# RMS norms over features: sums by f32r matmuls with a block of minus ones, roots by logarithm and exponential

## Chip, cores and metric

The kernel runs on one NeuronCore (one of eight) of a Trainium2 chip. The metric is the device time of one execution in microseconds (us), the median of several runs; less is better.

## What is computed

Two sequences of 512 tokens with 1024 features go through two layers (a grouped 2-D Fourier mixing, then grouped-query attention with axial rotary positions), each followed by a squared-ReLU MLP with 4096 hidden units, and a final norm. Everything is float32. Each mixer, each MLP and the output has an RMS norm over the features in front:

```python
def rms_norm(x, g):
    x32 = x.astype(jnp.float32)
    y = x32 * lax.rsqrt(jnp.mean(x32 * x32, axis=-1, keepdims=True) + EPS)
    return (y * g.astype(jnp.float32)).astype(x.dtype)

def sq_relu_mlp(h, w_up, w_down):
    a = jnp.maximum(h @ w_up, 0)
    return (a * a) @ w_down

def trunk(x, ...):
    for i in range(DEPTH):
        j = i // N_MIXERS
        if i % N_MIXERS == 0:
            x = x + fourier_mix(rms_norm(x, fourier_norm[j]), fourier_w_out[j])
        else:
            x = x + gqa_attention(rms_norm(x, attn_norm[j]), ...)
        x = x + sq_relu_mlp(rms_norm(x, mlp_norm[i]), mlp_w_up[i], mlp_w_down[i])
    return rms_norm(x, final_norm)
```

In attention the queries and keys of each head have an RMS norm of their own, over 128 features.

## The kernel before

The residual is held in SBUF with the features on partitions and the tokens along the free axis: for each sequence q eight tiles `xt(q, fo)` of 128 features by 512 tokens. A product in float32 precision is made of three f32r matmuls: both operands are split into a high part (a cast on ScalarE, `split`, line 86) and a low part (a subtraction on VectorE, line 87), and the products high x high, high x low and low x high add up in PSUM (`mm3`, lines 81 to 83; `product`, line 940, for the MLP).

The MLP uses a Strassen-like scheme: `Blocks` holds normalised pieces of both sequences (`b11`, `b21`, `b22`) and their sums and differences (`t1` to `t4`). `first_product` goes over pairs of weight blocks; for the first few (`AHEAD`) pairs only the products with the plain pieces run (`pair.first` with sequence 0, `pair.second`), while the second sequence's norm is finished, and `rest` then makes the products with the sums. `second_product` is the way down, from line 1131.

A norm over features needs a sum over partitions. Before the change it runs so:

- `square` (line 173) squares each feature tile on ScalarE (line 178) and adds it on GpSimd (line 182) into `acc[q]`; one tile can stand `apart`.
- `sums` (line 185) multiplies each block of 128 tokens of `acc` as the stationary operand with two columns of ones (line 191), in float32. The sums lie with tokens on partitions, one column for each block.
- `rsqrt_steps` (line 136) takes the reciprocal root of these few columns: a scaled copy (line 141), Sqrt on ScalarE (142), a reciprocal (143), a square (144) and one Newton step in two combined operations (145, 146).
- `spread` (line 195) transposes each column, broadcast to 128 columns, back with TensorE (line 199), so that each partition holds the row of factors, and copies it from PSUM (line 200).
- `Blocks.norm` (line 238) or `OutT.write` (line 1873) multiplies the scaled pieces (`gain`, lines 225 and 1862) by that row.

`Blocks` does this for both sequences in layer 0 (after the Fourier mixing: lines 884 and 887 for sequence 0, in `first_product` at lines 1069 and following for sequence 1) and in layer 1 (lines 1809 and following, and again `first_product`). `OutT` does it for the final norm of sequence 0 (`oa`, four token blocks) and of half of sequence 1 (`ob`, two blocks); the rest of sequence 1 (`oc`, `oe`) is transposed first and uses sums along the free axis (`Out`). Two more users of `sums` are the per-token scales of attention (`token_scale`, line 1402). `norm_rope` (line 1465) makes the norms of heads, with `rsqrt_steps` on VectorE or `log_steps` on GpSimd. Sqrt and Exp come from different tables on ScalarE; tables are loaded at lines 352, 1702 and 1741.

All engines take their instructions in the order that the program gives in these stretches (`manual_schedule`) or that a scheduler with added dependencies (`behind`) gives elsewhere. SyncE issues most loads and the spills; spills of the plain pieces are issued by ScalarE.

Of the kernel before, what the change touches and what calls it, by code (L numbers as in the profile page):

```python
# [44 lines left out]
def trunk_kernel(ctx, tc, x_in, xt_in, y_out, tables, rope, gfour, gcol, grow, gfin,  # L45
# [86 lines left out]
    def rsqrt(out, ss, n, inv, room=None):  # L132
        for step in rsqrt_steps(out, ss, n, inv, room=room):
            step()
# [16 lines left out]
    def log_steps(out, ss, n, inv):  # L151

        v, s, r, t = [small(n)[:, :n] for _ in range(4)]
        return [
            lambda: nc.vector.tensor_scalar(v, ss, inv, EPS, ALU.mult, ALU.add),
            lambda: nc.scalar.activation(s, ss, AF.Ln, scale=inv, bias=eps[:, :1]),
            lambda: nc.scalar.activation(r, s, AF.Exp, scale=-0.5),
            lambda: nc.vector.tensor_mul(t, r, r),
            lambda: nc.vector.scalar_tensor_tensor(t, t, -0.5, v, ALU.mult, ALU.mult),
            lambda: nc.vector.scalar_tensor_tensor(out, t, 1.5, r, ALU.add, ALU.mult),  # L160
        ]
# [23 lines left out]
    def sums(q, n=NT):  # L185

        o = ps()
        parts = [acc[q]] + ([apart.pop(q)] if q in apart else [])
        for t in range(n):
            for i, x in enumerate(parts):  # L190
                nc.tensor.matmul(o[:, 2 * t : 2 * t + 2], x[:, t * P : (t + 1) * P], ones,  # L191
                                 start=i == 0, stop=i == len(parts) - 1)
        return o[:, 0 : 2 * n : 2], o[:, 64:]

    def spread(r, n=NT):

        o, rows = ps()[:, : n * P], tm()
        for t in range(n):
            nc.tensor.transpose(o[:, t * P : (t + 1) * P], r[:, t : t + 1].broadcast_to([P, P]), ident)  # L199
        nc.scalar.copy(rows[:, : n * P], o)  # L200
        return rows
# [12 lines left out]
    class Blocks:  # L214
# [12 lines left out]

        def root(self, q):
            self.r[q] = small()
            ss, room = sums(q)  # L230
            rsqrt(self.r[q][:, :NT], ss, NT, 1.0 / D, room)

        def spread(self, q):
            self.rows[q] = spread(self.r[q])
# [140 lines left out]
    nc.vector.memset(f32(filler), 1.0)  # L375
    def cosT(c):
        return tabs[2 * c][:, :516].rearrange("p (a b) -> p a b", a=2)
# [355 lines left out]
    with tc.manual_schedule(engines={ET.PE, ET.Activation, ET.DVE, ET.Pool, ET.SP}):  # L733
# [116 lines left out]
        g1.chain(2, 6)  # L850
        even(4)
# [24 lines left out]
        for fo in range(KC):  # L876
            e, = even_outs(1, [fo])
            even_add(1, fo, e)
            if fo < 4:
                for i in range(2 * fo, 2 * fo + 2):  # L880
                    blocks.gain(0, i)
                if fo != 2:
                    put_away(0, fo)
            if fo == 2:
                blocks.root(0)
            if fo == 3:
                blocks.spread(0)
            if 3 < fo:
                blocks.first(fo - 4)
            if 5 < fo:  # L890
                blocks.first_lo(fo - 6)
# [53 lines left out]
    def first_product(l, blocks, rows, ahead):  # L945
# [122 lines left out]
        for p in range(AHEAD):  # L1068
            if p == 4:
                blocks.spread(1)  # L1070
            pair = pairs[p]
            if p < len(rows):
                pair.row = rows[p]
            else:
                pair.load()
                pair.split_row()
                if p == 3 and wo_added:
                    behind(pair.low, wo_added[0])
            pair.first()
            if p == 3:  # L1080
                blocks.root(1)
            if p > 0:
                pair.second()
            if p == 1:
                pairs[0].second()
            if p > 3:
                for _ in range(3):
                    next(todo)
            if p == 5:
                pairs[0].load_sums()  # L1090
                pairs[0].sums_13()
                pairs[0].sum_2()
            if p == 6:
                pairs[0].split_23()
# [307 lines left out]
    def token_scale(q):  # L1402
        r = sm.tile([P, NT], F32, tag="rs", name=nm("rs"), bufs=2)
        ss, room = sums(q)
        rsqrt(r, ss, NT, 1.0 / D, room)
# [49 lines left out]
    def norm_rope(raw, nh, table, ts, outs, ss=None, step=None, eng=nc.vector, scale=None):  # L1455
# [9 lines left out]
        steps = (log_steps if eng is nc.gpsimd else rsqrt_steps)(r[:, :n], ss[:, :n], n, 1.0 / HD)  # L1465
# [234 lines left out]
    with tc.manual_schedule(engines={ET.Activation}):  # L1700
        o = qkv(1, 1, 2, ws[1])
        tc.keep_in_program_order(nc.scalar.preload_act_table_set("natural_log_exp_and_others"))
# [12 lines left out]
    for n in range(1, len(heads) + 1):  # L1715
# [14 lines left out]
        last = nxt[-1] if nxt else last  # L1730
# [10 lines left out]
    behind(nc.scalar.activation(one[:, :1], last[:, :1], AF.Sqrt), both[0])  # L1741

# [14 lines left out]
    with tc.manual_schedule(engines={ET.PE}):  # L1757
# [38 lines left out]
        o, lows = {}, []  # L1796
        for j, (m, i) in enumerate(turn()):
# [11 lines left out]
            if j == 0:  # L1809
# [24 lines left out]
    class Out:  # L1834
# [9 lines left out]
        def root(self, i):  # L1844

            more = small(1)[:, 0:1]
            steps = rsqrt_steps(self.r, self.ss[:, i : i + 1], 1, 1.0 / D, more)
# [5 lines left out]
    class OutT:  # L1853


        def __init__(self, q, n):
            self.q, self.n, self.r, self.y = q, n, small(n), []
# [7 lines left out]
        def root(self):  # L1865
            ss, room = sums(self.q, self.n)
            rsqrt(self.r[:, : self.n], ss, self.n, 1.0 / D, room)

        def spread(self):
            self.rows = spread(self.r, self.n)[:, : self.n * P]  # L1870
# [15 lines left out]
    with tc.manual_schedule(engines={ET.PE, ET.Activation, ET.DVE, ET.Pool, ET.SP}):  # L1886
# [6 lines left out]
        for fo in range(KC):  # L1893
# [3 lines left out]
            if fo == 1:  # L1897
                oa.root()
# [29 lines left out]
        o = [tile(2, 0, 512, 2, ob.root)]  # L1928
        add(x, o[0], 0, 512)
        gain(x, y[0], 0)  # L1930
        o.append(tile(2, 512, 1024, 0, ob.spread))
# [189 lines left out]
```

## Time and profile before

| | |
|---|---|
| median of 3 runs | 1672.49 us (1672.36 to 1672.57) |
| span of the profiled execution | 1671.3 us |
| around the span, against the median | 1.2 us |
| TensorE busy | 1661.9 us, 99% |
| TensorE weight loads | 1387.8 us, 83% |
| VectorE busy | 1267.0 us, 76% |
| ScalarE busy | 872.1 us, 52% |
| GpSimd busy | 394.3 us, 24% |

Busy time is the sum of the durations; those of matmuls overlap, so the distance between the starts of two matmuls says what one costs. In a timeline row the first number is the start from the beginning of the span, the second the duration; `xN` joins N like instructions, and a bracket at the end gives the idle time before and what ended it. A matmul in float32 shows as two records, one in f32r as one.

### The profile page before, as it was taken

The page shows a single profiled execution, that of the slowest core. Times are in us where ns is not written, and L with a number is a line of the kernel's source. Part 1 is how long each engine was busy: PE and PEld are TensorE (multiplying, and loading weights), DVE is VectorE, ACT ScalarE, POOL GpSimd, SP SyncE. Part 2 cuts the span into 40 slices and gives each one's busy share as a digit, 9 for nine tenths or more (in the row PEclk, how much of TensorE's full clock was granted, in tenths as well). Part 3 has the DMA queues.
Part 4 walks back from the last instruction along what each step waited for, and adds up shares of the span by engine and source line. Part 5 has one row for each costly group of instructions (what it writes and reads, how often), then busy time and mean ns, then how long its engine had stood idle before and what let it go on. Part 6 is the DMA issues. An engine that isn't in the chain of part 4 may idle for free.

```text
span 1671.3 us, 22288 instructions
## 1 busy us (share of the span) xinstructions
PE 1661.9 (99%) x7843; PEld 1387.8 (83%) x7843; DVE 1267.0 (76%) x1851; ACT 872.1 (52%) x1540; POOL 394.3 (24%) x364
## 2 busy tenths in 40 slices
PE   9999999999999999999999999999999999999998
PEld 8988887888888888888888888888888888888887
DVE  8879776557886869869888877777855487878875
ACT  7766444446342435447688855554454552433334
POOL 3321444221000001325444303004422220000002
PEclk9999999999999999999999999999999999999999
DMA  9843554449775757425501156334544696757532
GB/s 306 257 158 118 204 195 172 151 170 373 250 228 165 248 170 236 168 77 200 166 1 39 64 176 223 117 120 167 211 145 166 221 375 194 233 158 236 178 104 101
DMA packets 122192, 302.48 MB, mean 181 GB/s; under 512 B 12344, under 2 KB 13496, under 8 KB 122080
## 3 DMA queue, kind: packets, MB, share of 16 engines
q1 hardware_dynamic: 98720, 253.53, 43.9%
q0 software_dynamic: 8960, 21.05, 6.0%
q10 hardware_dynamic: 14400, 26.48, 4.2%
q8 instruction: 61, 1.00, 0.2%
q14 instruction: 51, 0.42, 0.1%
HBM read 217.59 MB, written 82.38 MB: 179 GB/s over the span
## 4 chain that ended last, share of the span: by engine, by line
PE 97%; DVE 1%; DMA 0%; ACT 0%; issue 0%; POOL 0%; DVEq 0%; POOLq 0%; ACTq 0%
PE ps L940 74%; PE ps L83 6%; PE ps L81 6%; PE ps L82 6%; PE ps L1535 2%; PE ps L576 0%; PE ps L1514 0%; DMA raw<-w_up 0%; PE ps L191 0%; PE ps L507 0%; PE ps L504 0%; DVE w L87 0%; DVE raw L990 0%; PE ps L199 0%; DVE raw L989 0%
## 5 line engine op out<-in xcount | busy, mean ns | idle before, releaser
L940 PE MATMUL ps<-u,w 128*128 128x512 f32 x4944 | 1130.9, 389 | 1.2 <-DVE t L1018 1.2
L940 PEld LDWEIGHTS ps<-u,w 128*128 128x128 f32 x4944 | 926.6, 188 | 195.9 <-ACT u L973 1.7
L86 ACT CAST w<-raw 128x1024 fp32r<-128x1024 f32 (+1 forms) x216 | 213.7, 994 | 311.5 <-PE ps L940 234.3
L87 DVE TENSOR_TENSOR w<-raw,w 128x1024 fp32r<-128x1024 f32 (+1 forms) x216 | 252.0, 1170 | 75.7 <-ACT w L86 75.4
L86 ACT CAST u<-u 128x1024 fp32r<-128x1024 f32 x144 | 145.0, 1047 | 85.1 <-PE ps L940 36.4
L87 DVE TENSOR_TENSOR u<-u,u 128x1024 fp32r<-128x1024 f32 x144 | 174.3, 1239 | 17.3 <-ACT u L86 16.0
L940 PE MATMUL ps<-u,u 128*128 128x512 f32 x600 | 143.3, 389 | 0.0
L1150 DVE TENSOR_TENSOR u<-ps,u 128x512 f32<-128x512 f32 x160 | 109.9, 688 | 39.8 <-PE ps L940 37.3
L1177 POOL DMA_DIRECT2D raw<-w_sum x32 | 27.7, 865 | 468.2 <-DMA raw<-w_sum 170.8
L1058 POOL TENSOR_TENSOR u<-u 128x512 f32<-128x512 f32 x28 | 37.0, 1321 | 425.9 <-ACT u L955 425.9
L940 PEld LDWEIGHTS ps<-u,u 128*128 128x128 f32 x600 | 112.5, 188 | 24.1 <-ACT u L973 0.4
L81 PE MATMUL ps<-u,u 128*128 128x512 f32 (+2 forms) x340 | 128.7, 380 | 0.0
L83 PE MATMUL ps<-u,u 128*128 128x512 f32 (+2 forms) x340 | 123.7, 365 | 0.0
L82 PE MATMUL ps<-u,u 128*128 128x512 f32 (+2 forms) x340 | 123.6, 365 | 0.0
L182 POOL TENSOR_TENSOR t<-t,t 128x512 f32<-128x512 f32 (+1 forms) x54 | 79.2, 1470 | 187.0 <-ACT t L178 186.1
L954 ACT ACTIVATE t<-t 128x512 f32<-128x512 f32 x64 | 40.5, 632 | 109.2 <-DVE t L1027 95.7
L83 PEld LDWEIGHTS ps<-u,u 128*128 128x128 f32 x340 | 64.2, 189 | 10.5 <-DVE u L87 0.3
L87 DVE TENSOR_TENSOR u<-ps,u 128x512 fp32r<-128x512 f32 (+3 forms) x112 | 68.2, 636 | 5.6 <-ACT u L86 5.0
L82 PEld LDWEIGHTS ps<-u,u 128*128 128x128 f32 x340 | 64.4, 189 | 8.5 <-DVE u L87 0.3
L81 PEld LDWEIGHTS ps<-u,u 128*128 128x128 f32 x340 | 64.4, 189 | 7.8
L1014 DVE TENSOR_TENSOR t<-ps,u 128x512 f32<-128x512 f32 x32 | 22.0, 689 | 59.5 <-PE ps L940 55.8
L86 ACT CAST u<-ps 128x512 fp32r<-128x512 f32 (+3 forms) x112 | 59.5, 557 | 7.7 <-PE ps L1535 6.1
(270 smaller groups left out, 2024.6 us busy)
## 6 DMA issues: line engine op xcount, KB each, us to landing
raw<-w_up SPq DMA_DIRECT2D x80, 512.0 KB, 4.6
u<-spill_t SPq DMA_DIRECT2D x60, 512.0 KB, 6.7
raw<-w_sum SPq DMA_DIRECT2D x56, 512.0 KB, 5.5
u<-spill_b SPq DMA_DIRECT2D x45, 512.0 KB, 6.3
spill_t<-u SPq DMA_DIRECT2D x84, 256.0 KB, 2.0
spill_b<-t ACTq DMA_DIRECT2D x60, 256.0 KB, 4.4
raw<-w_row SPq DMA_DIRECT2D x28, 512.0 KB, 5.0
park<-u SPq DMA_DIRECT2D x24, 512.0 KB, 4.6
```

The source lines that it names most:

```text
L81: nc.tensor.matmul(out, lh, rh, start=first, stop=False)
L82: nc.tensor.matmul(out, lh, rl, start=False, stop=False)
L83: nc.tensor.matmul(out, ll, rh, start=False, stop=last)
L86: hi = nc.scalar.copy(dst_hi, src)
L87: return hi, eng.tensor_sub(dst_lo, src, f32(dst_hi))
L182: nc.gpsimd.tensor_add(acc[q][:, :n], acc[q][:, :n], s[:, :n])
L940: nc.tensor.matmul(o, w[x][:, sl], h[k][y], start=first and k + i == 0, stop=k == n - 1 and i == 2, skip_group_check=not first)
L954: nc.scalar.activation(t, src, AF.Relu)
L1058: eng.tensor_sub(t[:, 0], b12, b11)
L1150: return nc.vector.tensor_add(x, o, x)
L1177: nc.gpsimd.dma_start(s[:, 1], w[:, 3], accum_op=ALU.add)
L1535: nc.tensor.transpose(pt[:, t * P : (t + 1) * P], probs[t][:, sc * P : (sc + 1) * P], ident)
```

## The change

The sums of the six feature norms are made by f32r matmuls: the accumulated squares are split into a high and a low half like any operand (class `Rows`, `split`), and a 128x128 block of minus ones (one column, broadcast) is the stationary operand. All 128 partitions then hold minus the sum for each token, and no transposes are needed. ScalarE takes Ln (scale -1/D) and Exp (scale -0.5) over the whole width and a Square, and two combined operations on VectorE make the Newton step. The splitting, the root and the last step each have a place of their own in the program. The smaller roots (`token_scale`, `norm_rope`, `Out.root`) also use Ln and Exp in place of Sqrt and a reciprocal; only the first roots in the setup keep Sqrt. The table with Ln and Exp is loaded once, early, and the two later table loads go.

```diff
-    def rsqrt(out, ss, n, inv, room=None):
-        for step in rsqrt_steps(out, ss, n, inv, room=room):
+    def rsqrt(out, ss, n, inv):
+        for step in log_steps(out, ss, n, inv):
             step()
...
-    def log_steps(out, ss, n, inv):
+    def log_steps(out, ss, n, inv, more=EPS):
...
+        def root():
+            nc.scalar.activation(r, ss, AF.Ln, scale=inv, bias=eps[:, :1] if more is EPS else more)
+            nc.scalar.activation(r, r, AF.Exp, scale=-0.5)
...
-        return o[:, 0 : 2 * n : 2], o[:, 64:]
-
-    def spread(r, n=NT):
-
-        o, rows = ps()[:, : n * P], tm()
-        for t in range(n):
-            nc.tensor.transpose(o[:, t * P : (t + 1) * P], r[:, t : t + 1].broadcast_to([P, P]), ident)
-        nc.scalar.copy(rows[:, : n * P], o)
-        return rows
+        return o[:, 0 : 2 * n : 2]
+
+    class Rows:
+        def __init__(self, q, n=512):
+            self.q, self.n, self.parts = q, n, []
+
+        def split(self, x):
+            h = slot([P, 2, self.n], F32R)
+            made = split(h[:, 0], h[:, 1], x[:, : self.n])
+            self.parts += [h[:, 0], h[:, 1]]
+            return made
+
+        def split_all(self):
+            for x in [acc[self.q]] + ([apart.pop(self.q)] if self.q in apart else []):
+                made = self.split(x)
+            return made
+
+        def root(self):
+            n, o = self.n, ps()
+            self.o, room = o[:, :n], slot([P, 2, n], F32)
+            self.x, self.t = room[:, 0], room[:, 1]
+            for i, x in enumerate(self.parts):
+                nc.tensor.matmul(self.o, minus[:, :1].broadcast_to([P, P]), x, start=i == 0, stop=i == len(self.parts) - 1)
+            nc.scalar.activation(self.x, self.o, AF.Ln, scale=-1.0 / D, bias=eps[:, :1])
+            nc.scalar.activation(self.x, self.x, AF.Exp, scale=-0.5)
+            nc.scalar.activation(self.t, self.x, AF.Square, scale=(0.5 / D) ** 0.5)
+
+        def rows(self):
+            nc.vector.scalar_tensor_tensor(self.t, self.o, -D * EPS, self.t, ALU.add, ALU.mult)
+            out = tm((P, self.n))
+            nc.vector.scalar_tensor_tensor(out, self.t, 1.5, self.x, ALU.add, ALU.mult)
+            return out
...
+    minus = cons.tile([P, 2], F32R, name="minus")
+    nc.gpsimd.memset(f32(minus), -1.0)
...
         g1.chain(2, 6)
+        nc.scalar.preload_act_table_set("natural_log_exp_and_others")
...
             e, = even_outs(1, [fo])
+            if fo == 2:
+                blocks.split_sums(0)
             even_add(1, fo, e)
+            if fo == 3:
+                blocks.root(0)
...
-            if fo == 2:
-                blocks.root(0)
-            if fo == 3:
+            if fo == 4:
                 blocks.spread(0)
...
             pair.first()
+            if p == 2:
+                blocks.split_sums(1)
             if p == 3:
                 blocks.root(1)
...
-        steps = (log_steps if eng is nc.gpsimd else rsqrt_steps)(r[:, :n], ss[:, :n], n, 1.0 / HD)
+        steps = log_steps(r[:, :n], ss[:, :n], n, 1.0 / HD)
...
-        tc.keep_in_program_order(nc.scalar.preload_act_table_set("natural_log_exp_and_others"))
...
-    behind(nc.scalar.activation(one[:, :1], last[:, :1], AF.Sqrt), both[0])
...
+        blocks.split_sums(0)
         for j, (m, i) in enumerate(turn()):
...
-            if j == 0:
+            if j == 1:
                 blocks.root(0)
...
             if fo == 1:
-                oa.root()
+                oa.r.split_all()
+            if fo == 2:
+                oa.r.root()
             if fo == 3:
                 oa.spread()
...
-        o = [tile(2, 0, 512, 2, ob.root)]
+        ob.r.split_all()
+        o = [tile(2, 0, 512, 3, ob.r.root)]
         add(x, o[0], 0, 512)
         gain(x, y[0], 0)
-        o.append(tile(2, 512, 1024, 0, ob.spread))
+        ob.spread()
+        o.append(tile(2, 512, 1024))
```

The lines of the changed kernel lie some 30 to 36 higher: line 940 becomes 976, 238 becomes 269, 1873 becomes 1903. How instructions move is shown at three places.

VectorE in layer 0, the second sequence's norm, in `first_product`; before (w are halves of weights, line 238 the normalisation):

```order
L993 TENSOR_TENSOR raw_1631<-raw_1629,raw_1627 128x512
L87 TENSOR_TENSOR w_1541<-raw_1539,w_1541 128x1024
L87 TENSOR_TENSOR w_1585<-raw_1583,w_1585 128x1024
L141 TENSOR_SCALAR s_1510<-ps_1505 128x4
L143 RECIPROCAL s_1511<-ps_1505 128x4
L87 TENSOR_TENSOR w_1637<-raw_1635,w_1637 128x1024
L145 SCALAR_TENSOR_TENSOR ps_1505<-ps_1505,s_1510 128x4
L146 SCALAR_TENSOR_TENSOR s_1504<-ps_1505,s_1511 128x4
L87 TENSOR_TENSOR w_1683<-raw_1631,w_1683 128x1024
L238 TENSOR_TENSOR u_1224<-u_1224,t_1533 128x1024
L238 TENSOR_TENSOR u_1309<-u_1309,t_1533 128x1024
```

and now (lines 227 and 229 are the two wide combined operations, u_1470 is the low half of the sums):

```order
L87 TENSOR_TENSOR u_1470<-t_1196,u_1470 128x512
L87 TENSOR_TENSOR w_1528<-raw_1526,w_1528 128x1024
L87 TENSOR_TENSOR w_1572<-raw_1570,w_1572 128x1024
L87 TENSOR_TENSOR w_1624<-raw_1622,w_1624 128x1024
L227 SCALAR_TENSOR_TENSOR u_1503<-ps_1502,u_1503 128x512
L229 SCALAR_TENSOR_TENSOR t_1524<-u_1503 128x512
L87 TENSOR_TENSOR w_1670<-raw_1618,w_1670 128x1024
L269 TENSOR_TENSOR u_1219<-u_1219,t_1524 128x1024
```

The low half comes ahead of four weight halves; the four small operations are gone, and two wide ones stand ahead of the last weight half and the normalisation.

ScalarE in the final norms, sequence 0 (`oa`) while the projection of sequence 1 runs; before (lines 178 and 1862 are the square and the gain of a tile of 256 tokens):

```order
L178 ACTIVATE t_14618<-u_12368 128x256
L1862 ACTIVATE u_14620<-u_12368,gc 128x256
L178 ACTIVATE t_14636<-u_12368 128x256
L1862 ACTIVATE u_14620<-u_12368,gc 128x256
L142 ACTIVATE ps_14640<-ps_14640,eps 128x4
L144 ACTIVATE ps_14640<-s_14646 128x4
L178 ACTIVATE t_14667<-u_12559 128x256
L1862 ACTIVATE u_14670<-u_12559,gc 128x256
L178 ACTIVATE t_14686<-u_12559 128x256
```

and now (lines 182 and 1896 are the square and the gain):

```order
L182 ACTIVATE t_14565<-u_12317 128x256
L1896 ACTIVATE u_14567<-u_12317,gc 128x256
L182 ACTIVATE t_14583<-u_12317 128x256
L1896 ACTIVATE u_14567<-u_12317,gc 128x256
L86 CAST u_14587<-t_14392 128x512
L182 ACTIVATE t_14604<-u_12508 128x256
L1896 ACTIVATE u_14607<-u_12508,gc 128x256
L222 ACTIVATE u_14610<-ps_14609,eps 128x512
L223 ACTIVATE u_14610<-u_14610 128x512
L224 ACTIVATE u_14610<-u_14610 128x512
```

The cast of the sums stands behind the second tile's gain, and Ln, Exp and Square (222 to 224) behind the third tile's.

TensorE in the final norms, `ob`, in the first tiles of the last tokens (ps_14780 and ps_14808 before, ps_14726 and ps_14753 now); before:

```order
L83 MATMUL ps_14780<-w_14413,u_14392 128x512
L191 MATMUL ps_14790<-ones,t_14618 128x2
L191 MATMUL ps_14790<-ones,t_14773 128x2
L191 MATMUL ps_14790<-ones,t_14618 128x2
L191 MATMUL ps_14790<-ones,t_14773 128x2
L81 MATMUL ps_14780<-w_14418,u_14397 128x512
L82 MATMUL ps_14780<-w_14418,u_14397 128x512
L83 MATMUL ps_14780<-w_14418,u_14398 128x512
L81 MATMUL ps_14808<-w_14403,u_14379 128x512
L82 MATMUL ps_14808<-w_14403,u_14379 128x512
L83 MATMUL ps_14808<-w_14403,u_14380 128x512
L199 MATMUL ps_14812<-ident,s_14426 128x128 x2
```

and now:

```order
L83 MATMUL ps_14726<-w_14367,u_14347 128x512
L221 MATMUL ps_14739<-u_14720,minus 128x256 x2
L221 MATMUL ps_14739<-u_14723,minus 128x256 x2
L81 MATMUL ps_14753<-w_14352,u_14328 128x512
L82 MATMUL ps_14753<-w_14352,u_14328 128x512
L83 MATMUL ps_14753<-w_14352,u_14329 128x512
```

The sums stood ahead of the tile's last three matmuls and the transposes behind the first three of the next; the new matmuls stand between the two tiles.

## Rows read from the trace of the kernel before

**Rows 1.** The page, parts 1 and 4: busy time; the chain by engine.

```profile
PE 1661.9 (99%) x7843; PEld 1387.8 (83%) x7843; DVE 1267.0 (76%) x1851; ACT 872.1 (52%) x1540; POOL 394.3 (24%) x364
...
PE 97%; DVE 1%; DMA 0%; ACT 0%; issue 0%; POOL 0%; DVEq 0%; POOLq 0%; ACTq 0%
```

**Rows 2.** List of TensorE's waits: us in total, times, longest.

```profile
PE ps L576 <- DVE mask L369: 1.2, 1, 1.2
PE ps L940 <- DVE t L1018: 1.2, 1, 1.2
```

**Rows 3.** Stretches: us; busy (count) of PE, PEld, DVE, ACT, POOL; PEclk; DMA.

```profile
116.00:150.00 34.00, 34.00 (x150) 27.68 (x149) 32.82 (x34) 21.16 (x30) 0.00 (x0) 1.00 0.27 96
...
1031.00:1051.00 20.00, 19.99 (x88) 16.23 (x88) 20.00 (x17) 13.69 (x19) 10.10 (x6) 1.00 0.31 109
...
1066.00:1101.00 35.00, 35.00 (x154) 28.34 (x153) 32.95 (x32) 22.71 (x32) 0.00 (x0) 1.00 0.26 89
```

**Rows 4.** Timeline of PE, layer 0's first norm: start, us, line.

```profile
70.05 0.95 PE L191 MATMUL ps<-ones,t 128*128 128x2 f32 x8
70.86 0.36 PE L81 MATMUL ps<-u,w 128*128 128x258 f32 x1
71.06 0.28 PE L82 MATMUL ps<-u,w 128*128 128x258 f32 x1
71.18 0.28 PE L83 MATMUL ps<-u,w 128*128 128x258 f32 x1
```

**Rows 5.** Timeline of PE, layer 1's first norm.

```profile
1020.58 1.84 PE L191 MATMUL ps<-ones,t 128*128 128x2 f32 x16
1022.28 0.49 PE L940 MATMUL ps<-u,w 128*128 128x512 f32 x1
```

**Rows 6.** Timeline of PE, layer 0's second norm: the spread.

```profile
113.90 0.62 PE L199 MATMUL ps<-ident,s 128*128 128x128 f32 x4 [0.23 <-DVE s L146]
114.28 1.41 PE L940 MATMUL ps<-u,w 128*128 128x512 f32 x5
```

**Rows 7.** The page, part 5: MLP matmuls.

```profile
L940 PE MATMUL ps<-u,w 128*128 128x512 f32 x4944 | 1130.9, 389 | 1.2 <-DVE t L1018 1.2
```

**Rows 8.** ScalarE's groups by form: count, busy, mean ns.

```profile
L1527 ACT ACTIVATE t<-ps,s 128x512 f32<-128x512 f32 x64 | 44.8, 701 | 4.1 <-DVE s L1525 2.3 <-DVE s L1528 1.7
...
L178 ACT ACTIVATE t<-u 128x512 f32<-128x512 f32 x56 | 34.6, 630 | 40.0 <-DVE u L1747 21.0 <-DVE u L924 12.9 <-DVE w L87 2.3
...
L86 ACT CAST u<-t 128x512 fp32r<-128x512 f32 x33 | 20.3, 616 | 2.0 <-DVE u L87 1.1 <-ACT t L955 0.8
```

**Rows 9.** VectorE's groups by form: a low half.

```profile
L87 DVE TENSOR_TENSOR u<-t,u 128x512 fp32r<-128x512 f32 x33 | 22.7, 687 | 0.0
```

**Rows 10.** Timeline of ACT: the second late table load.

```profile
962.22 1.28 ACT L1741 ACT_TABLE_LOAD   x1
963.51 0.20 ACT L1741 ACTIVATE s<-t 128x1 f32<-128x1 f32 x1
```

**Rows 11.** Timeline of ACT, layer 0's second norm.

```profile
113.71 0.60 ACT L954 ACTIVATE u<-ps 128x512 f32<-128x512 f32 x1 [1.42 <-PE ps L940]
```

**Rows 12.** Timeline of DVE, the same place: the normalisation.

```profile
116.41 2.36 DVE L238 TENSOR_TENSOR u<-u,t 128x1024 f32<-128x1024 f32 x2
```

**Rows 13.** Timeline of ACT behind the full stretch.

```profile
148.84 2.00 ACT L86 CAST w<-raw 128x1024 fp32r<-128x1024 f32 x2 [1.30 <-DVE raw L993]
```

**Rows 14.** Timeline of PE there.

```profile
150.07 1.78 PE L940 MATMUL ps<-u,w 128*128 128x512 f32 x7
```

**Rows 15.** Timeline of ACT in the final norms: a gain.

```profile
1643.27 0.49 ACT L1862 ACTIVATE u<-u,gc 128x256 f32<-128x256 f32 x1
```

**Rows 16.** Timeline of PE in the final norms.

```profile
1642.23 0.95 PE L191 MATMUL ps<-ones,t 128*128 128x2 f32 x8
...
1655.84 0.40 PE L81 MATMUL ps<-w,u 128*128 128x512 f32 x1
```

**Rows 17.** Timeline of DVE there: blocks of the output.

```profile
1648.39 1.22 DVE L1873 TENSOR_TENSOR u<-u,t 128x1024 f32<-128x1024 f32 x1
...
1653.23 1.43 DVE L1873 TENSOR_TENSOR u<-u,t 128x1024 f32<-128x1024 f32 x1
```

More of the change, by code (lines that the diff above doesn't have):

```diff
@@ L147, in rsqrt_steps @@
         ]
-    def log_steps(out, ss, n, inv):
-        v, s, r, t = [small(n)[:, :n] for _ in range(4)]
+    def log_steps(out, ss, n, inv, more=EPS):
+        v, r, t = [small(n)[:, :n] for _ in range(3)]
+        def root():
+            nc.scalar.activation(r, ss, AF.Ln, scale=inv, bias=eps[:, :1] if more is EPS else more)
+            nc.scalar.activation(r, r, AF.Exp, scale=-0.5)
         return [
-            lambda: nc.vector.tensor_scalar(v, ss, inv, EPS, ALU.mult, ALU.add),
-            lambda: nc.scalar.activation(s, ss, AF.Ln, scale=inv, bias=eps[:, :1]),
-            lambda: nc.scalar.activation(r, s, AF.Exp, scale=-0.5),
+            lambda: nc.vector.tensor_scalar(v, ss, inv, more, ALU.mult, ALU.add),
+            root,
             lambda: nc.vector.tensor_mul(t, r, r),
@@ L226, in gain, with split_sums @@
                                  scale=gc[:, self.g0 + fo : self.g0 + fo + 1])
+        def split_sums(self, q):
+            self.r[q] = Rows(q)
+            return self.r[q].split_all()
         def root(self, q):
-            self.r[q] = small()
-            ss, room = sums(q)
-            rsqrt(self.r[q][:, :NT], ss, NT, 1.0 / D, room)
+            self.r[q].root()
         def spread(self, q):
-            self.rows[q] = spread(self.r[q])
+            self.rows[q] = self.r[q].rows()
         def norm(self, q, i):
@@ L1403, in token_scale @@
         r = sm.tile([P, NT], F32, tag="rs", name=nm("rs"), bufs=2)
-        ss, room = sums(q)
-        rsqrt(r, ss, NT, 1.0 / D, room)
+        rsqrt(r, sums(q), NT, 1.0 / D)
         rs.append(r)
@@ L1729, in trunk_kernel @@
                     next(todo, None)
-        last = nxt[-1] if nxt else last
         if n + 1 < len(heads):
@@ L1846, in root @@
             more = small(1)[:, 0:1]
-            steps = rsqrt_steps(self.r, self.ss[:, i : i + 1], 1, 1.0 / D, more)
+            steps = log_steps(self.r, self.ss[:, i : i + 1], 1, 1.0 / D, more)
             if i > 1:
@@ L1856, in __init__ @@
         def __init__(self, q, n):
-            self.q, self.n, self.r, self.y = q, n, small(n), []
+            self.q, self.n, self.r, self.y = q, n, Rows(q, n * P), []
         def gain(self, fo):
@@ L1863, in gain @@
                                  scale=gc[:, 3 * KC + fo : 3 * KC + fo + 1])
-        def root(self):
-            ss, room = sums(self.q, self.n)
-            rsqrt(self.r[:, : self.n], ss, self.n, 1.0 / D, room)
         def spread(self):
-            self.rows = spread(self.r, self.n)[:, : self.n * P]
+            self.rows = self.r.rows()
         def write(self, i):
```

## The prediction

> **What bounds the kernel now.** I read the page first. TensorE is busy for 1661.9 of 1671.3 us and its work makes up 97% of the chain that ended last [rows 1]. The list of TensorE's waits names only two of over a microsecond [rows 2]: nearly everything else runs behind matmuls. So a microsecond taken from TensorE's own instructions can come off the time, but only as far as the operands of later matmuls also come earlier. The view by stretches shows where they may not: in three of them VectorE has no room left, 32.82 of 34 us, 20.00 of 20, and 32.95 of 35, each just behind a place that the change touches, while the granted clock stands at 1.00, the 2.4 GHz level [rows 3]. Then the timelines of single engines give prices and slack. What counts as a result: 0.2% is 3.3 us, about what a measurement of this kernel can tell from no change.
>
> **TensorE's sum.** Durations overlap on this engine, so I count from start to start. The eight records of a sum (line 191) begin at 70.05, the next matmul at 70.86, and its successor 0.20 later where 0.12 is usual: 0.81 + 0.08 = 0.89 us [rows 4]. Four more such groups go, 5 x 0.89 = 4.45, and the group of sixteen, from 1020.58 to 1022.28, is 1.70 + 0.08 = 1.78 [rows 5]. (The two groups for the per-token scales stay.) Four spread transposes (line 199) take 0.38 to the next start plus the same 0.08, 0.46; five groups of four and one of two give 2.5, and one of them waited 0.23 for VectorE [rows 6]. Removed: 4.45 + 1.78 + 2.5 + 0.23 = 9.0 us. Added are twelve matmuls of 512 columns and four of 256. A 512-column matmul costs 1130.9 / 4944 = 0.229 us [rows 7], a 256-column one about the 0.12 of its 258-column neighbours [rows 4]: 2.75 + 0.48 = 3.2. The balance is -5.8 us. Per place: 0.9 and 1.1 in layer 0, 1.3 and 0.9 in layer 1, 0.9 and 0.6 in the final norms (rounded).
>
> The Trainium skill, TensorE: Matmul & The Clock Gate (section on 56 ns against 53.3 ns), has warm matmuls start every N / 2.4 GHz + 2.5 ns; by that estimate the added ones cost 3.0 us and the balance would be 6.0. The row is the slower and decides.
>
> **VectorE, ScalarE and GpSimd.** A site's chain was four small VectorE operations, a root, a square and a 512-column copy. It becomes, on ScalarE, a cast (0.62), Ln and Exp (nearest row an Exp from PSUM, 0.70) and a Square (0.63) [rows 8], on VectorE a low half and two wide combined operations, each priced at the low half's 0.69 [rows 9]; as neither wide operation shows before, I allow 0.4 to 1.1 for it. That is about 1.3 us more on each engine. On the per-head norms VectorE loses a reciprocal and ScalarE gains an Exp on a few columns; both stand in an attention part where TensorE waits for almost nothing [rows 2], so I take 0 with 0.5 either way. GpSimd gains one memset in the setup; neither of TensorE's two waits is for GpSimd [rows 2], so I take 0, and at most the one memset if it held up the constants. SyncE's order of loads is unchanged.
>
> Table loads: two go, one comes at about 50 us. The load at 962.22 takes 1.28 us and the next activation starts at 963.51 with no idle time [rows 10]; both old loads lie where TensorE does not wait, so 0. The new one meets ScalarE in the setup, where TensorE also does not wait: 0, at most its own 1.28. The Trainium skill, ScalarE: Activation LUTs (What ACT_TABLE_LOAD costs), puts a switch at 1.28 us plus a drain of 1.38, 2.66 us in all; the trace shows no such drain, before or behind. By the page the removed loads would free more of ScalarE, and the time would still not follow.
>
> **What survives at each place.**
> - *Layer 0, first norm*: the operand is used much later, so 0.9 stays. *Second norm*: the DVE rows of the order show the two wide operations ahead of the last weight half and the normalisation. ScalarE's step that starts this waits for TensorE at 113.71 [rows 11], which by then has gained 0.9 + 0.4; the normalisation at 116.41 [rows 12] so moves forward by about 1.3. VectorE is then full until a cast on ScalarE begins at 148.84 after the raw sums, ends a microsecond later, and the matmul that needs it starts at 150.07 [rows 13, 14]: 0.2 us of slack. TensorE arrives 2.0 earlier, the operand 1.3 earlier. I take 1.3, with 0 (the stretch starts no earlier) and 2.0 as ends.
> - *Layer 1*: the first norm frees 1.3 on TensorE, but the full stretch 1031 to 1051 follows [rows 3]; its chain hangs on a weight cast and on wide operations, so I pass on 0.7 (0 to 1.3). The second norm frees 0.9, its chain starts early enough, and I keep all of it (0 to 0.9). Together 1.6.
> - *The final norms* cost rather than pay. The cast for the first stands behind the gain that ends at 1643.27 + 0.49 = 1643.76 [rows 15]; plus 0.62 and 0.69 the low half is there at 1645.1. TensorE, without the sum that began at 1642.23 [rows 16], arrives after twelve more matmuls of 0.12, at 1643.7, and stands still for 1.2 us after using the high half: with the last matmul, it is at 1645.3 where it was at 1643.7 + 0.9 = 1644.6. Minus 0.46 for the transposes it is 0.3 late. Then Ln, Exp, Square and two wide operations (3.4 us) follow, and the first output block that VectorE wrote at 1648.39 starts near 1649.5. Four writes and the sums between them leave no gap, so the last ends at 1655.75 where it ended at 1653.23 + 1.43 = 1654.66 [rows 17]. Only then come two low halves of 256 columns, about 0.4 each, and the last minus-ones matmul ends near 1656.6. Before, the next tile's first matmul began at 1655.84 [rows 16], and a spread of two transposes (0.2) followed: 1656.6 - 1655.84 - 0.2, or 0.5 late in all (ends: the 1.5 gained that TensorE's sum gives, 1.3 lost if the wide work comes on top). What ends the kernel, a matmul and then the sums behind it, moves with TensorE.
>
> Sum: 1.3 + 1.6 - 0.5 = 2.4 us saved. The profiled execution has a span of 1671.3; the median, 1672.5, is 1.2 above, and I keep that distance: 1671.3 - 2.4 + 1.2 = **1670.1 us**, 0.14% below, which is inside what counts as no change.
>
> **Rivals.**
> 1. *TensorE's whole saving arrives*: 1672.5 - 5.8 = 1666.7. For it speaks that nothing but TensorE stands in the chain; against it, the full VectorE of rows 3 and a slack of 0.2. Chance 0.2.
> 2. *The holds take everything*: each place gives TensorE a wait as long as what it lost, and the time stays at 1672.5, give or take 0.5. For it: a slack of 0.2 at 150.07. Against: the stretches before it start on TensorE's own events. Chance 0.1.
> 3. *Slower: the wide operations land in the full stretches.* The point that decides is whether the first normalisation behind a root starts later than now, at 116.41 in layer 0 (and near 1031 in layer 1). If 1.3 us of wide work delays it instead of the lead moving it forward, layer 0 loses 1.3 - 0.2 = 1.1, layer 1 1.3 and the second low half of 0.7, 2.0, and the end 0.5 + 1.3 = 1.8: 4.9 in all, 1677.4. Against: VectorE idles in front of these places. Chance 0.1, of which 0.03 stay under 3.3 us.
> 4. *The roots' table swap matters*: the load at 50 us on TensorE's path costs 1.28, time 1671.3. It lies inside the forecast's range and has no chance of its own beyond 0.02 of the forecast's.
>
> **How the numbers follow.** The forecast has 0.6, its own range 1668.6 to 1671.5; 0.12 of that is under 1669.15, the bound of 0.2%. Faster: 0.2 + 0.12 = 0.32. Slower: 0.07. Within: 0.61. The range runs from 1666.6, just below the first rival's time, to 1673.4, past the second's; that leaves out the third rival's 0.1 and about 0.05 below.
>
> **What would show it.** TensorE's busy time should fall by about 6 us, the two lines 191 and 199 to sixteen records, and new waits of TensorE should appear at the first late matmuls after the full stretches (about 0.7 each near 149 and 1047) and at both new groups of the end (1 us each), in all near 3 us. If the normalisation behind the second root of layer 0 begins before 115.5, that step is right; if it begins after 116.4, rival 3 has it. If the waits list stays as short as now, rival 1 was true. I would be wrong altogether if a wait appears in the attention part or in the setup.

## The result, and the profile of the changed kernel

| | before | changed |
|---|---|---|
| median | 1672.57 us (1672.08 to 1673.74, 12 runs) | 1676.25 us (1674.52 to 1677.55, 12 runs) |
| ratio | | 1.002, interval 1.0012 to 1.0027 |
| span of the profiled execution | 1671.3 us [rows 1] | 1674.1 us (its own time 1675.87) |

The change costs 3.7 us between the medians (0.2%). The prediction, 1670.1 with a range to 1673.4, lies on the wrong side. The page of the changed kernel, busy times and the chain that ended last, against [rows 1]:

```profile
PE 1658.6 (99%) x7781; PEld 1382.4 (83%) x7781; DVE 1266.9 (76%) x1823; ACT 884.3 (53%) x1570; POOL 395.0 (24%) x365
...
PE 91%; DVE 6%; ACT 2%; issue 1%; DMA 1%; POOL 0%; DVEq 0%; ACTq 0%; POOLq 0%
```

TensorE is busy for 3.3 us less, and the time is still longer: 6% of the chain is now VectorE's, where it was 1%, or 2% in a second trace of the old kernel. The list of TensorE's waits (us in total, times, longest) says where, against [rows 2]:

```profile
PE ps L976 <- DVE w L87: 2.6, 3, 1.4
PE ps L221 <- ACT u L86: 1.2, 2, 0.7
PE ps L609 <- DVE mask L400: 1.2, 1, 1.2
PE ps L976 <- DVE u L1780: 0.8, 1, 0.8
PE ps L390 <- DMA g<-gfour: 0.6, 1, 0.6
PE ps L976 <- DVE t L1063: 0.6, 1, 0.6
PE ps L976 <- ACT u L1009: 0.5, 1, 0.5
PE ps L976 <- DVE t L1188: 0.4, 1, 0.4
PE ps L221 <- DVE u L87: 0.4, 2, 0.2
```

Line 976 is the MLP's product, 221 the new minus-ones matmul; line 609's wait is line 576's of before. The first line, 2.6 us for low halves of weights, is the largest, and no step of the prediction has it. The same stretches of the changed kernel as in [rows 3] (columns as there), with one more ahead of them that the prediction left out:

```profile
74.70:97.20 22.50, 22.50 (x165) 21.21 (x164) 21.83 (x35) 15.29 (x22) 6.67 (x4) 1.00 0.69 247
116.00:150.00 34.00, 32.84 (x144) 26.61 (x143) 33.90 (x35) 20.99 (x29) 0.00 (x0) 1.00 0.31 108
1031.00:1051.00 20.00, 18.75 (x81) 14.84 (x81) 20.00 (x17) 13.82 (x19) 8.57 (x5) 1.00 0.27 104
1066.00:1101.00 35.00, 33.58 (x149) 27.44 (x148) 33.44 (x33) 21.85 (x31) 0.00 (x0) 1.00 0.25 86
```

In the three stretches of [rows 3] TensorE had next to no idle time; now it has 1.16, 1.25 and 1.42 us. VectorE is as full as it was or a little fuller: 33.90 in the first, where the old kernel's two traces have 32.82 and 33.46, and 33.44 in the last, for 32.95 and 33.38. TensorE does not run slower, it stands: the granted clock is 1.00 throughout. Its timeline at the places where it stands (the bracket is the idle time before the row's first matmul):

```profile
100.59 1.67 PE L976 MATMUL ps<-u,w 128*128 128x512 f32 x6 [0.60 <-DVE w L87]
...
129.67 1.65 PE L976 MATMUL ps<-u,w 128*128 128x512 f32 x6 [0.59 <-DVE w L87]
...
148.66 2.98 PE L976 MATMUL ps<-u,u 128*128 128x512 f32 x12 [0.56 <-DVE t L1063]
...
1038.78 3.04 PE L976 MATMUL ps<-u,w 128*128 128x512 f32 x12 [0.78 <-DVE u L1780]
...
1047.74 4.62 PE L976 MATMUL ps<-u,u 128*128 128x512 f32 x19 [0.48 <-ACT u L1009]
...
1081.98 2.37 PE L976 MATMUL ps<-u,w 128*128 128x512 f32 x9 [1.42 <-DVE w L87]
...
1645.78 0.50 PE L221 MATMUL ps<-u,minus 128*128 128x512 f32 x1 [0.50 <-ACT u L86]
...
1657.69 0.38 PE L221 MATMUL ps<-u,minus 128*128 128x256 f32 x1 [0.75 <-ACT u L86]
```

Counting matmuls in their order, I compared the start of each with the same one's in a second trace of the old kernel (below). The difference falls where the old sums and transposes are gone and rises at these waits (in us; numbers in brackets are places in the changed kernel's trace):

| stretch | saved | given back | net |
|---|---|---|---|
| layer 0, first norm | 0.9 | 1.1 (97, 100) | +0.2 |
| layer 0, second norm | 1.3 | 1.6 (129, 148, 151) | +0.3 |
| layer 1, first norm | 1.2 | 1.4 (1038, 1047) | +0.2 |
| layer 1, second norm | 1.1 | 1.5 (1081) | +0.4 |
| final norms | 2.3 | 3.5 (1645, 1657) | +1.1 |

In the first four rows the added matmuls are taken off "saved"; in the last they stand, with 0.9 us, in "given back", so that by the count of the others it is 1.4 and 2.6. The rest of 3.1 us (1674.1 - 1671.0, the second trace) is 0.3 at the first load, 0.4 at a load near 1520, which no run here ties to the change, and 0.2 behind the last matmul. Attention and setup are as they were. So the saving is where it was forecast, and each place hands back a little more than it got.

### The profile page after: what moved, and what is told of

It is laid out like the page before. It is cut to its first block, busy times and chain, and to the rows that moved or that the text cites. A ratio compares the mean times of both kernels' runs of the same rounds, so it can differ in the third digit from the quotient of the medians.

```text
span 1674.1 us, 22156 instructions
## 1 busy us (share of the span) xinstructions
PE 1658.6 (99%) x7781; PEld 1382.4 (83%) x7781; DVE 1266.9 (76%) x1823; ACT 884.3 (53%) x1570; POOL 395.0 (24%) x365
## 4 chain that ended last, share of the span: by engine, by line
PE 91%; DVE 6%; ACT 2%; issue 1%; DMA 1%; POOL 0%; DVEq 0%; ACTq 0%; POOLq 0%
PE ps L976 70%; PE ps L83 6%; PE ps L81 6%; PE ps L82 6%; PE ps L1572 2%; DVE u L87 1%; DVE u L269 1%; DVE u L1903 0%; DVE w L87 0%; DVE u L286 0%; PE ps L1551 0%; ACT w L86 0%; DMA raw<-w_sum 0%; PE ps L540 0%; PE ps L609 0%
## 5 line engine op out<-in xcount | busy, mean ns | idle before, releaser
L1530 POOL TENSOR_TENSOR u<-t,t 128x256 f32<-128x256 f32 x40 | 49.7, 1255 | 63.0 <-DVE t L1528 45.1
```

The lines of the kernel that those rows point to most:

```text
L1530: nc.gpsimd.tensor_add(outs[(h0 + i) // 2].rearrange("p (h d) -> p h d", h=2), t1[:, i : i + 2], t2[:, i : i + 2])
```

## Experiments

Each is an edit of the changed kernel. Medians stand beside that of the old kernel in the same set of runs: 1673.0 for `all_cols`, `blocks_cols`, `tail_cols` and `no_newton`; 1673.2 for `nn_square`, `double_stt`, `tail_moved` and `nn_tail`; 1673.3 for `nn_stt`, `nn_a0`, `nn_tail2` and `before_again`. For the changed kernel's own set it is 1672.57, so a difference between medians of two sets is uncertain by up to 0.7 us. Where that matters, I give the difference a second time, each median first taken against the old kernel of its own set ("against the old kernels"). Three theories: **V** (theory W in the recorded expectations), the wide work of the Newton step stands in VectorE's full stretches; **S**, the small roots with their tables cost the time; **T**, the final norms alone cost it.

### Which part costs: three partial undos

`all_cols` puts all six feature norms back to column sums and transposes at their old places, and keeps the new small roots and the early table:

```diff
+    class Cols:
...
+        def root(self):
+            n = self.n // P
+            self.r = small(n)
+            rsqrt(self.r[:, :n], sums(self.q, n), n, 1.0 / D)
...
-            self.r[q] = Rows(q)
+            self.r[q] = (Cols if self.g0 // (2 * KC) * 10 + q in (0, 1, 10, 11,) else Rows)(q)
...
-        oa, ob, oc, oe = OutT(0, 4), OutT(1, 2), Out(2), Out(3)
+        oa, ob, oc, oe = OutT(0, 4, Cols), OutT(1, 2, Cols), Out(2), Out(3)
```

`blocks_cols` does so for the four norms of the layers alone, `tail_cols` for the two final ones alone.

> All six feature norms go back to sums in columns and transposes, at their old places; the logarithm and exponential in all small roots, the early table and the absent late tables stay. Theory W (the wide operations delay stretches in which VectorE is full, and TensorE gives its saving back in waits): the cost is gone, 1672.5 us within 0.7. Theory S (the small roots and the tables cost the time, in attention and in the setup): 1675.5 to 1676.5, as in the changed kernel.

> Only the two final norms keep the new sums; the four norms of the layers go back to columns. Theory W: in the trace of the changed kernel TensorE's lag behind the old one grows by 1.3 us from 1640 us to the end, so 1673.8 within 0.5. Theory S: 1675.5 to 1676.5.

> The reverse: only the four norms of the layers keep the new sums. Theory W: the remaining part of the 3.7 us, 1674.9 within 0.7. Theory S: 1675.5 to 1676.5. If a start of the execution that was 0.9 us late in the changed kernel's trace belongs to the program, it shows here too.

Measured: `all_cols` 1672.92 us, ratio 1.0 (0.9991 to 1.0009); `blocks_cols` 1674.51, 1.001 (1.0001 to 1.0019); `tail_cols` 1673.93, 1.0005 (0.9996 to 1.0014). **S falls**: the swapped roots and table loads are worth nothing that these runs can tell (the interval is 1.5 us either way). With the new final norms alone the time is 1.6 above `all_cols`, with the new layer norms alone 1.0, and with both 3.3 (1676.25 - 1672.92; 3.8 against the old kernels); the parts sum to 2.6. T falls as the only cause: with the layer norms undone (`blocks_cols`) the time is 1.7 below the changed kernel's (2.2 against the old kernels). Two of the three missed: `blocks_cols` came out above the range that V gave it (1673.3 to 1674.3), `tail_cols` below its own. But the list of waits of `tail_cols` has the changed kernel's waits of the layers again and neither of the two lines for line 221:

```profile
PE ps L998 <- DVE w L87: 2.9, 4, 1.4
...
PE ps L998 <- DVE u L1802: 0.8, 1, 0.8
PE ps L998 <- DVE t L1085: 0.6, 1, 0.6
PE ps L998 <- ACT u L1031: 0.5, 1, 0.5
```

### Without the wide work

`no_newton` leaves out the Newton step at the six feature norms: the Square and both combined operations.

```diff
-            nc.scalar.activation(self.t, self.x, AF.Square, scale=(0.5 / D) ** 0.5)
...
-            nc.vector.scalar_tensor_tensor(self.t, self.o, -D * EPS, self.t, ALU.add, ALU.mult)
-            out = tm((P, self.n))
-            nc.vector.scalar_tensor_tensor(out, self.t, 1.5, self.x, ALU.add, ALU.mult)
-            return out
+            return self.x
```

> The Newton step of the six feature norms is left out (the Square on ScalarE and both wide combined operations on VectorE), so the factors are those of the exponential alone. Theory W: 1.3 us of VectorE and 0.6 of ScalarE go at each place, the normalisations behind begin 1.3 to 2 us earlier, and the time falls by 3 to 5 us, to 1671 to 1673. Theory S: no change, 1675.5 to 1676.5. A third, that the cast and the low half in front of the new sums are what holds: a fall of under 1.5 us.

Measured: 1668.31 us (1667.74 to 1669.07), ratio 0.9971 (0.996 to 0.9982): 7.9 below the changed kernel and 4.7 below the old one. It fell further than expected. TensorE's waits in the layers are gone but for one of 0.2 us; the list of its waits for `no_newton` begins:

```profile
PE ps L605 <- DVE mask L396: 1.2, 1, 1.2
PE ps L221 <- ACT u L86: 0.5, 1, 0.5
PE ps L386 <- DMA g<-gfour: 0.5, 1, 0.5
```

and its stretches, as above, show TensorE full again and VectorE with room:

```profile
116.00:150.00 34.00, 34.00 (x150) 27.64 (x149) 32.39 (x33) 21.88 (x30) 0.00 (x0) 1.00 0.25 89
1031.00:1051.00 20.00, 20.00 (x90) 16.43 (x89) 17.61 (x16) 13.47 (x20) 8.08 (x5) 1.00 0.52 168
1066.00:1101.00 35.00, 34.78 (x152) 28.08 (x151) 31.17 (x33) 22.90 (x31) 0.00 (x0) 1.00 0.22 73
```

So the Newton step is what costs, as V has it, and the split sums by themselves bring most of what they promise: 4.7 of 5.8 us. The stand at the first final norm (line 221, 0.5 for the cast and 0.2 for the low half) is there without the Newton step too.

### Which of the three operations

`nn_square` is `no_newton` with ScalarE's Square kept, its result unused; `nn_stt` is `no_newton` with one wide combined operation on VectorE for each norm, its result unused; `double_stt` is the changed kernel with the second combined operation made twice at the five norms of 512 tokens.

```diff
+            nc.vector.scalar_tensor_tensor(self.t, self.x, 1.5, self.x, ALU.add, ALU.mult)
             return self.x
```

```diff
             nc.vector.scalar_tensor_tensor(out, self.t, 1.5, self.x, ALU.add, ALU.mult)
+            if self.n == 512:
+                nc.vector.scalar_tensor_tensor(out, self.t, 1.5, self.x, ALU.add, ALU.mult)
```

> No Newton step, as in no_newton, but ScalarE still makes the Square (nobody reads it). If VectorE's two wide operations are what cost: 1668.3 within 0.7, as no_newton. If ScalarE's length of chain costs as well: 1669.5 to 1671.

> No Newton step, but one wide combined operation on VectorE at each of the six places (its result is not used). With nn_square (ScalarE alone) this divides the 8 us that the step cost. Theory W, all of it from VectorE in line: half of the way from 1668.3 to 1676.3, so 1671 to 1673. If the length of the chain through both engines is what costs: under 1 us more than no_newton.

> The changed kernel with the last wide combined operation made twice where it is 512 wide (five places), 0.7 us more of VectorE each; the output is the same. Theory W: VectorE is full behind these places, so most of 5 x 0.7 = 3.5 arrives: 2 to 3.5 us more than the changed kernel, 1678.3 to 1679.8. Rival (VectorE has room, ScalarE or the split in front holds): under 1 us more.

Measured: `nn_square` 1670.19 us, 1.9 above `no_newton` (1.7 against the old kernels), in the range for a ScalarE chain that counts too; its interval, 0.9972 to 0.999, overlaps that of `no_newton`, so the size is loose. `nn_stt` 1670.88, just under its range and 2.6 above `no_newton` (2.3), for five operations of about 0.7 and one of half the width, some 3.8 us of VectorE. `double_stt` 1677.67, 1.4 above the changed kernel, but 0.8 against the old kernels: well under the 2 to 3.5 that V gave it, and at or near its rival's "under 1 us". Five of its seven executions have a mean granted clock of 0.998, where all of the changed kernel have 0.999 (the last section shows what happened in the profiled one); the two others took 1676.67 and 1677.03. So `double_stt` does not speak for V. A Square at 1.9 and two combined operations at 2.6 each make 7.1 of the 7.9 that the Newton step cost (6.3 of 8.4 against the old kernels). V names VectorE's part, which is the larger; ScalarE's Square seems to cost as well. What one such operation does is seen in `nn_stt`, in the list of TensorE's waits; no wait of this kind stands in that of `no_newton`:

```profile
PE ps L973 <- DVE w L87: 1.4, 1, 1.4
```

### Layer 0's first norm alone

`nn_a0` leaves the Newton step out at this one norm.

```diff
+            self.r[q].newton = self.g0 > 0 or q > 0
...
+            if not self.newton:
+                return self.x
```

> The changed kernel with the Newton step left out at one place only, the first norm of layer 0, of which the prediction said that it costs nothing. Theory W: VectorE is full from that norm on, so its normalisation begins 1.3 us or more earlier and TensorE's wait near 99.6 us (0.8) goes, and part of those behind it up to 151 us: 0.8 to 1.8 us less than the changed kernel, 1674.5 to 1675.5. If the prediction's step was right (hidden): no change, 1676.2.

Measured: 1674.83 us, ratio 1.001 (1.0002 to 1.0019), 1.4 below the changed kernel (2.1 against the old kernels): this norm was not hidden, though the two intervals overlap and the size is loose. The wait at 100 is gone from its trace. Not foreseen: a longer stand of TensorE appears further on, from its timeline

```profile
130.65 7.57 PE L980 MATMUL ps<-u,w 128*128 128x512 f32 x25 [1.95 <-ACT u L86]
```

and behind it the granted clock falls (columns as [rows 3]):

```profile
132.20:135.60 3.40, 3.40 (x10) 2.64 (x9) 3.40 (x4) 1.72 (x2) 0.00 (x0) 0.51 0.37 140
135.60:140.00 4.40, 4.40 (x21) 3.66 (x20) 3.70 (x4) 3.43 (x5) 0.00 (x0) 1.00 0.27 76
```

Half a clock for 3.4 us costs about 1.7 us of this execution, by my estimate. Its mean granted clock is 0.998, as in three other executions of the eleven, and these four are the slowest, 1675.12 to 1676.72; the seven with 0.999 took 1674.13 to 1674.97.

### The final norms, earlier or later

`tail_moved` puts the matmuls and the last step of `oa` two tiles of the projection earlier; `nn_tail` is that with `no_newton`; `nn_tail2` moves `ob`'s matmuls three matmuls later as well, into the second tile.

```diff
+        oa.r.split_all()
...
-            if fo == 1:
-                oa.r.split_all()
-            if fo == 2:
+            if fo == 0:
                 oa.r.root()
-            if fo == 3:
+            if fo == 1:
                 oa.spread()
```

> The changed kernel with one move: for the first final norm the sums are split before the tokens are transposed, the new matmuls stand behind the first feature tile of the projection instead of the third, and the last step behind the second. Theory W: TensorE's wait of about 1.2 us at the first of the two new groups of the end goes and the output blocks start earlier: 1.2 to 2 us less than the changed kernel, 1674.3 to 1675.1. Rival: the wait comes back at the second group, under 0.5 us less.

> No Newton step, and the move of tail_moved. In the trace of no_newton TensorE lost 1.65 us at the first group of the end; with it moved ahead 1 to 1.6 us less than no_newton: 1666.7 to 1667.3. Rival: output blocks and the second group hold instead, 1668.3.

> nn_tail with one more move: the new matmuls of the last norm stand behind the first three matmuls of the second tile of the last tokens, instead of between the tiles. In the trace of nn_tail TensorE lost about 0.6 us there: 0.3 to 0.6 us less than nn_tail, 1667.4 to 1667.7. Rival: VectorE's last blocks come later and hold the end, no gain.

Measured: `tail_moved` 1674.96 us, 1.3 below the changed kernel (1.9 against the old kernels), in its range; `nn_tail` 1667.99, ratio 0.9969 (0.9957 to 0.998), only 0.3 below `no_newton` (0.5), which is short of its range and less than these runs can tell; `nn_tail2`, ratio 0.9971 (0.996 to 0.9982), no gain over `nn_tail`. `nn_tail` has the lowest time of all, below both kernels, but without the refinement of the root. For `tail_moved` the number came as expected and the reason did not. The stand at `oa`'s group, 0.50 and 0.23 in the changed kernel, should have gone; it is 0.36 and 0.23. `ob`'s grew from 0.75 and 0.15 to 1.01. Counted matmul by matmul, its trace gains nothing on the changed kernel's from 1640 to the end; the two differ at the first load and near 1520. What made its median lower stays open. The list of TensorE's waits in `tail_moved`, line 221:

```profile
PE ps L221 <- ACT u L86: 1.4, 2, 1.0
```

### The old kernel once more

`before_again` is the old kernel unchanged, for a second trace.

> The old kernel unchanged, for a second trace. If the wait of 1.2 us at 258.7 and the early landing of the first load (3.0 us after its issue) belong to the program they are there again; if they are chance, the wait is gone and the landing takes 3.5 to 3.9 us as in all the other traces. The time is 1672.5 to 1673 either way.

Measured: 1672.8 us with a span of 1671.0. TensorE's waits in the second trace of the old kernel:

```profile
PE ps L576 <- DVE mask L369: 1.2, 1, 1.2
PE ps L359 <- DMA g<-gfour: 0.4, 1, 0.4
PE ps L199 <- DVE s L146: 0.2, 1, 0.2
PE ps L1535 <- POOL t L1529: 0.2, 1, 0.2
```

The wait for line 1018 in [rows 2] is not there: it was of that one execution. The wait for the first load, here 0.4 and in the changed kernel 0.6, is not the change's either.

## Why the prediction was wrong

- **TensorE's own sum, -5.8 us: right.** The savings in the table, less the added matmuls, make 5.9, and `no_newton`, which has every new matmul, keeps 4.7 us of it against the old kernel. TensorE's busy time fell by only 3.3, where the prediction gave about 6 as a sign: beside a stand the matmuls start further apart (the place at 100.59 costs 0.87 us with an idle time of 0.60), and busy time counts that. The tables and the small roots at 0: right, as far as `all_cols` can tell (ratio 1.0). Attention and setup without a new wait: right. The prediction wrote of two waits, neither for GpSimd; the old kernel's list also has one of 0.2 for GpSimd, and the changed kernel's has the same.
- **"Layer 0, first norm: the operand is used much later, so 0.9 stays": the step that failed first.** I took only three places to have a full stretch behind them, and the first norm to have room. The old kernel's stretch there is as full as the others:

```profile
74.70:97.20 22.50, 22.50 (x164) 21.38 (x164) 21.83 (x36) 15.02 (x20) 8.13 (x5) 1.00 0.69 251
```

  VectorE works for 21.83 of 22.5 us while TensorE never waits. The two combined operations at 75.65 and 76.37 therefore come out again 24 us later, when a low half of weights, which began at 96.85, begins at 98.51, and TensorE, which runs through here in the old kernel, stands for 0.60 at 99.99. (In the second trace of the old kernel it began at 97.68, still without a wait of TensorE; so of the 1.7 us only 0.8 are beyond what one execution differs from another, and `nn_a0` has to decide.) VectorE's timeline, old kernel:

```profile
96.85 1.96 DVE L87 TENSOR_TENSOR w<-raw,w 128x1024 fp32r<-128x1024 f32 x1 [0.32 <-ACT w L86]
```

  changed kernel (the idle time ends with a cast of ScalarE, which had itself waited for VectorE and came as much later):

```profile
75.65 0.68 DVE L227 SCALAR_TENSOR_TENSOR u<-ps,u 128x512 f32<-128x512 f32 x1
76.37 0.69 DVE L229 SCALAR_TENSOR_TENSOR t<-u 128x512 f32<-128x512 f32 x1
...
98.51 2.02 DVE L87 TENSOR_TENSOR w<-raw,w 128x1024 fp32r<-128x1024 f32 x1 [0.27 <-ACT w L86]
```

  and `nn_a0`, where the two are left out and it starts where it did in the old kernel:

```profile
96.87 2.01 DVE L87 TENSOR_TENSOR w<-raw,w 128x1024 fp32r<-128x1024 f32 x1 [0.28 <-ACT w L86]
```

- **"The normalisation at 116.41 so moves forward by about 1.3": wrong, and rival 3's deciding point.** In the changed kernel it begins at 118.17, 1.8 later than in [rows 12]; in `no_newton` at 114.17, 2.2 earlier. The prediction's mark of 116.4 was a weak one, as the old kernel's own second trace begins at 117.25; but the changed kernel is 0.9 later than that too, where 1.3 earlier was forecast. I had counted what TensorE gains ahead of the chain but not that the chain itself, Square and two wide operations, is longer than the small steps it replaces. VectorE's timeline of the changed kernel:

```profile
115.71 0.68 DVE L227 SCALAR_TENSOR_TENSOR u<-ps,u 128x512 f32<-128x512 f32 x1
116.43 0.69 DVE L229 SCALAR_TENSOR_TENSOR t<-u 128x512 f32<-128x512 f32 x1
...
118.17 2.35 DVE L269 TENSOR_TENSOR u<-u,t 128x1024 f32<-128x1024 f32 x2
```

  and of `no_newton`:

```profile
114.17 2.35 DVE L265 TENSOR_TENSOR u<-u,u 128x1024 f32<-128x1024 f32 x2
```

- **Layer 1: the gain of 1.6 came out as a loss of 0.6.** The first normalisation begins at 1031.80, where it began at 1030.76 (1029.94 in the second trace): the second combined operation took 1.78 us, not 0.69, beside an add of GpSimd (below). The second norm, of which I kept "all", lost 1.42 at 1081 to a low half of weights. VectorE's timeline, old kernel and then the changed one:

```profile
1030.76 1.85 DVE L238 TENSOR_TENSOR u<-u,t 128x1024 f32<-128x1024 f32 x1 [0.38 <-ACT t L200]
```

```profile
1031.80 3.46 DVE L269 TENSOR_TENSOR u<-u,t 128x1024 f32<-128x1024 f32 x2
```

- **The final norms: right in kind, mis-sized.** Predicted were stands of 1.2 and 1 us and a loss of 0.5; the timeline gives 0.7 and 0.9, TensorE loses 1.1 in the trace, and the runs say 1.6 (`blocks_cols` against `all_cols`). Behind the first group TensorE is 0.4 later, near the 0.3 forecast; the second adds 0.7, where 0.2 were forecast. The term's losing end, 1.3, was the better price: counted the same way, `no_newton` gains 0.15 over the end, so the wide work did come on top.
- **Rival 3** named the mechanism, the place and 1677.4 us; 1676.25 were measured. Its parts were each too dear: 1.1 for layer 0, 2.0 for layer 1 and 1.8 for the end, where the table has 0.5, 0.6 and 1.1. Its chance of 0.1 was too low: "VectorE idles in front of these places" was true of the moment, and not of the stretch behind. The waits forecast near 149 and 1047 came (0.56 and 0.48); those at 100, 129, 1038 and 1081 were not.

## What to carry to other kernels

Work moved off a saturated engine paid here only as far as the engine that took it had room over the whole stretch up to the next late operand, so make the table of stretches for every place that the change touches, and cut its limits at the places where the loaded engine has an idle gap. Work is priced by its width, and not by the number of operations: VectorE's four on four columns (0.17 us for a combined one) became two on 512 (0.69 each; on 256 at the last norm), and over the six norms these, with the Square, cost more than the sums and transposes gave (7.9 us for 5.9). A refinement step that stands in such a stretch is worth asking about first: without it the same change saves 4.7 us here, with it 3.7 are lost.

## What the runs showed of the hardware

- A combined operation with both operands in SBUF waited out an add of GpSimd that had begun before it. Timelines of the changed kernel, VectorE and GpSimd, layer 1 and then the final norms:

```profile
1029.50 1.78 DVE L229 SCALAR_TENSOR_TENSOR t<-u 128x512 f32<-128x512 f32 x1
...
1649.63 0.69 DVE L227 SCALAR_TENSOR_TENSOR u<-ps,u 128x512 f32<-128x512 f32 x1 [0.73 <-ACT u L224]
1650.35 0.97 DVE L229 SCALAR_TENSOR_TENSOR t<-u 128x512 f32<-128x512 f32 x1
```

```profile
1028.99 1.74 POOL L186 TENSOR_TENSOR t<-t,t 128x512 f32<-128x512 f32 x1 [2.75 <-ACT t L182]
...
1650.04 0.74 POOL L186 TENSOR_TENSOR t<-t,t 128x256 f32<-128x256 f32 x1 [1.86 <-ACT t L182]
```

  The adds end at 1030.73 and 1650.78, the combined operations 0.55 and 0.54 later: in both cases about the time of one undisturbed operation (0.69), less 0.14. The one at 1649.63, with an operand in PSUM, runs beside the same add and takes its usual 0.69. The other traces with the Newton step at these places (`tail_cols`, `blocks_cols`, `double_stt`, `nn_a0`, `tail_moved`) have 1.77 to 1.78 at the first and 0.92 to 0.98 at the second. The Trainium skill, SBUF — State Buffer (section on two separate sides), has such a VectorE operation and a GpSimd operation share a port pair by an exclusive lock, the loser blocked until the other ends; these two pairs agree with it.
- The granted clock can fall behind a single stand. In `nn_a0` it goes to 0.51 for 3.4 us after TensorE stood for 1.95, in `double_stt` to 0.50 from 1660.2 to 1663.5 after it stood for 1.48 at 1657; after the stands of 1.42 in the changed kernel and in `nn_stt` it stayed at 1.00. These are one execution each; 0.51 and 0.50 are the 1.2 GHz level. The stretch of `double_stt` (columns as [rows 3]):

```profile
1660.20:1663.50 3.30, 3.30 (x9) 2.55 (x8) 2.14 (x4) 1.67 (x5) 0.00 (x0) 0.50 0.27 108
```

  The Trainium skill, TensorE: Matmul & The Clock Gate (What's actually happening), also has two levels, 1.2 and 2.4 GHz, and the rows agree. What else sets the fall in these stretches was not tried.
